# Thirty instead of twenty-six pairs of an up projection by seven products, with nine plain pairs spread among them

## The chip, the cores and the metric

The kernel runs on one core of one Trainium2 chip. The metric is device time in microseconds (us) of one execution, median over runs: 2329.23 us for the kernel before (3 runs, 2329.02 to 2341.73). The engines are called by their short names: PE (TensorE, matmul; PEld is its weight load), DVE (VectorE), ACT (ScalarE), POOL (GpSimd), SP (SyncE, which here issues all DMAs).

## The reference

One decoder block over 512 tokens of width 2048: a modulated RMS norm, two token mixers with a shared output projection, then a gated MLP with a causal depthwise convolution of width 3, and a last norm. The change concerns the MLP's up projection alone:

```python
def _conv_ffn(h, w_up, conv_w, conv_b, w_down):
    T = h.shape[1]
    u = h @ w_up
    up = jnp.pad(u, ((0, 0), (CONV_WIDTH - 1, 0), (0, 0)))
    y = conv_b
    for j in range(CONV_WIDTH):
        y = y + conv_w[j] * up[:, j:j + T]
    val, gate = jnp.split(y, 2, axis=-1)
    return (jax.nn.silu(gate) * val) @ w_down
```

`h` is 512 x 2048, `w_up` is 2048 x 11264, `w_down` 5632 x 2048, all float32.

## The kernel before

All activations are kept transposed: 128 channels on the partitions, 512 tokens on the free axis. A product of float32 precision is made from three matmuls in a narrower format (`mm3`, lines 127 to 130): weight and activation are each split into a high part (a rounding cast, on ACT) and a low part (the difference, on DVE), and high by high, high by low and low by high are summed in PSUM. `split_weights` (lines 117 to 125) does this for a tile of 128 x 512 weights: one load on SP (`wraw`, 4 buffers), one cast (`whi`, 3 buffers, line 122), one difference (`wlo`, 3 buffers, line 124). `project` uses it for four k-tiles at a time.

The up projection has 44 pairs. A pair is 128 columns of the value half and 128 of the gate half. Each goes through `conv` (one ACT instruction and two on DVE, lines 851 to 853), then the gate's Silu on ACT (857), a product on DVE (858) and a store to `actd` in DRAM (859). They are made in three ways:

- the first NORD = 5 pairs in the ordinary way, before the stage in question;
- the next NSEV = 26 pairs by Strassen's seven products in place of eight (in the form with few additions). Tokens are halved (2 x 256), the contraction is halved (2 x 1024), and the pair's two column tiles are the third halving. The sums of the activations are made once (`token_sums`, `token_split`). The weights come in NPC = 4 chunks a pair, each of 2 k-tiles of each half;
- the last 13 pairs are plain ones, made by the generator `plain_tiles`: a pair is two tiles, a tile four quarters of four k-tiles, and `yield` stands after each quarter. A quarter is 12 matmuls of 512 columns. After a tile's fourth quarter its `conv` follows, after a pair's second tile the gate.

The stage is one loop over n, the NST = 4 x NSEV chunks (lines from 1032 on). In each turn it makes the sums of the next chunk's weights on POOL (`weight_sums`, lines 971 to 973), splits the next chunk's plain parts (`parts("p", ...)`: `ph` on ACT, line 983, `pl` on DVE, line 984), loads the raw weights of the chunk after it (line 965, 512 KB, 2 buffers), and splits this chunk's sums (`sh`, `sl`, the same lines), which are put behind the plain parts on ACT and DVE by `issue_after`. All these tiles have 2 buffers. Then PE makes three products on plain parts, one plain quarter, and the four products on sums; each product of a chunk is 6 matmuls of 256 columns. After a pair's fourth chunk `combine` (one ACT and seven DVE instructions, lines 998 to 1005) joins the seven results, and `gated` follows.

PSUM has eight banks of one pool: a pair's seven products take one each, the plain tile in progress one. Two tags are shared: the sums of the weights lie in `wraw` and `wlo` buffers. The order of instructions on each engine is fixed at compile time by a scheduler that follows the order in the program but moves an instruction that is ready ahead of one that is not; on the chip each engine takes its queue in that order.

Behind the stage stands the down projection: it loads the activations back (`ald`, from `actd`), and weights through `split_weights` (`wdn`), and reloads the residual tiles x from DRAM (line 1069, `x<-x2d`, into memory that the stage gives back).

The line that decides where a plain quarter goes is in the loop:

```python
        if n >= 2:
            next(others, None)
```

With 104 chunks and 104 quarters, each chunk from the third on has one, and the two that are left follow the loop.

Of the kernel before, what the change touches and what calls it, by code (L numbers as in the profile page):

```python
# [18 lines left out]
P = 128  # L19
T = 512  # L20
D = 2048
KT = D // P
NF = 44
# [5 lines left out]
WC = 512  # L29
# [2 lines left out]
Q = float(np.exp(-0.5))  # L32
WINS = (2, 4, 8, 16)
NORD = 5
NSEV = 26
NPC = 4
DK = 4

# [26 lines left out]
def block_kernel(ctx, tc, a, out, stop=None, dbg=None):  # L65
# [66 lines left out]
    def project(ps, src, acts, start=True, stop=True, engs=(V,)):  # L132

        n = len(acts)
        for k0 in range(0, n, WC // P):
            nk = min(WC // P, n - k0)
            wh, wl = split_weights(src[:, k0 * P : (k0 + nk) * P], engs[k0 // 4 % len(engs)])
            for kk in range(nk):
                k = k0 + kk
                sl = slice(kk * P, (kk + 1) * P)  # L140
                last = mm3(ps, wh[:, sl], wl[:, sl], *acts[k], start=start and k == 0, stop=stop and k == n - 1)
            beats.append(last.ins)
        return last
# [662 lines left out]
    def bank():  # L806
        return psm.tile([P, T], F32, tag="b", name="b")

    def half(acts, hf):
        sl = slice(hf * HT, (hf + 1) * HT)  # L810
        return [(h[:, sl], l[:, sl]) for h, l in acts]
# [37 lines left out]
    def conv(c, j, tag):  # L849
        y = rb.tile([P, T], F32, tag=tag, name=tag, bufs=2)  # L850
        S.activation(y, c, AF.Identity, bias=col("cb", j), scale=col("cw", 176 + j))
        V.scalar_tensor_tensor(y[:, 1:T], c[:, 0 : T - 1], col("cw", 88 + j), y[:, 1:T], op0=ALU.mult, op1=ALU.add)
        V.scalar_tensor_tensor(y[:, 2:T], c[:, 0 : T - 2], col("cw", j), y[:, 2:T], op0=ALU.mult, op1=ALU.add)
        return y

    def gate_pair(j, yv, yg):
        S.activation(yg, yg, AF.Silu)
        V.tensor_mul(yv, yv, yg)
        nc.sync.dma_start(actd[j], yv)

    def gated(j, cv, cg):
        gate_pair(j, conv(cv, j, "t0"), conv(cg, NF + j, "t1"))
# [100 lines left out]
    def load_four(n):  # L963
        raw = up.tile([P, 4, W2], F32, tag="raw", name="raw", bufs=2)
        nc.sync.dma_start(raw, a["wups"][n // NPC, n % NPC, :, :, :])
        return raw

    def weight_sums(raw):
        sa = wp.tile([P, WC], F32, tag="wraw", name="sums", bufs=4)[:, :].rearrange("p (n w) -> p n w", n=2)
        sb2 = wp.tile([P, WC], F32, tag="wlo", name="sums", bufs=3)[:, :].rearrange("p (n w) -> p n w", n=2)  # L970
        G.tensor_tensor(sa, raw[:, 1:3, :], raw[:, 0:1, :].to_broadcast([P, 2, W2]), op=ALU.add)  # L971
        G.tensor_tensor(sb2[:, 0, :], sa[:, 0, :], raw[:, 2, :], op=ALU.add)  # L972
        G.tensor_tensor(sb2[:, 1, :], sb2[:, 0, :], raw[:, 3, :], op=ALU.add)
        return sa, sb2

    def parts(tag, srcs):
        m = sum(t.shape[1] for t in srcs)
        hi = up.tile([P, m, W2], F32R, tag=tag + "h", name=tag + "h", bufs=2)
        lo = up.tile([P, m, W2], F32R, tag=tag + "l", name=tag + "l", bufs=2)
        n = 0  # L980
        for t in srcs:
            sl = slice(n, n + t.shape[1])
            act = S.copy(hi[:, sl, :], t)  # L983
            dve = V.tensor_tensor(lo[:, sl, :], t, hi[:, sl, :].bitcast(F32), op=ALU.subtract)  # L984
            n += t.shape[1]
        return [(hi[:, i, :], lo[:, i, :]) for i in range(m)], (act, dve)

    def product(q, c, w, xs_):
        for i in range(2):
            sl = slice(i * P, (i + 1) * P)  # L990
            mm3(q, w[0][:, sl], w[1][:, sl], *xs_[i], start=c == 0 and i == 0, stop=c == NPC - 1 and i == 1)

    def combine(q):
        cv = up.tile([P, T], F32, tag="cv", name="cv")
        cg = up.tile([P, T], F32, tag="cg", name="cg")
        u = up.tile([P, 3, HT], F32, tag="u", name="u")
        A1, B1 = slice(0, HT), slice(HT, T)
        S.copy(cg[:, A1], q[1])
        V.tensor_tensor(cv[:, A1], cg[:, A1], q[2], op=ALU.add)
        V.tensor_tensor(u[:, 0, :], cg[:, A1], q[6], op=ALU.subtract)  # L1000
        V.tensor_tensor(u[:, 1, :], u[:, 0, :], q[7], op=ALU.add)
        V.tensor_tensor(u[:, 2, :], u[:, 0, :], q[5], op=ALU.subtract)
        V.tensor_tensor(cg[:, B1], q[5], u[:, 1, :], op=ALU.subtract)
        V.tensor_tensor(cv[:, B1], u[:, 2, :], q[3], op=ALU.add)
        V.scalar_tensor_tensor(cg[:, A1], u[:, 1, :], -1.0, q[4], op0=ALU.mult, op1=ALU.subtract)
        return cv, cg

    def plain_tiles():
        for j in range(NORD + NSEV, NF):
            yv = None  # L1010
            for i in range(2):
                ps = bank()
                for k0 in range(0, KT, WC // P):
                    k1 = k0 + WC // P
                    project(ps, a["wup"][2 * (j - NSEV) + i - 4, :, k0 * P : k1 * P], H2[k0:k1],
                            start=k0 == 0, stop=k1 == KT)
                    if k1 == KT:
                        y = conv(ps, j + NF * i, f"t{i}")
                        if i:
                            gate_pair(j, yv, y)  # L1020
                        yv = y
                    yield

    NST = NSEV * NPC
    others = plain_tiles()
    raws = [load_four(0), load_four(1)]
    sums = weight_sums(raws[0])
    pw, _ = parts("p", [raws[0][:, 1:4, :]])
    q = {}
    for n in range(NST):  # L1030
        c = n % NPC
        if n + 1 < NST:
            raw = raws.pop()
            nsums = weight_sums(raw)
            npw, marks = parts("p", [raw[:, 1:4, :]])
            if n + 2 < NST:
                raws.append(load_four(n + 2))
        with tc.issue_after(marks[0].ins), tc.issue_after(marks[1].ins):
            sw, _ = parts("s", sums)
        (a22, a11, a12), (s1, s3, s2, s4) = pw, sw  # L1040
        ks = (2 * c, 2 * c + 1)
        b11, b21, b22 = half([H2[k] for k in ks], 0), half([H2[k + HK] for k in ks], 0), half([H2[k + HK] for k in ks], 1)
        t1, t2, t3, t4 = ([TK[k][i] for k in ks] for i in range(4))
        if c == 0:
            q = {}
        for m, w, xs_ in ((1, a11, b11), (2, a12, b21), (4, a22, t4)):
            if c == 0:
                q[m] = bank()[:, 0:HT]
            product(q[m], c, w, xs_)
        if n >= 2:  # L1050
            next(others, None)
        for m, w, xs_ in ((6, s2, t2), (7, s3, t3), (5, s1, t1), (3, s4, b22)):
            if c == 0:
                q[m] = bank()[:, 0:HT]
            product(q[m], c, w, xs_)
        if c == NPC - 1:
            gated(NORD + n // NPC, *combine(q))
        if n + 1 < NST:
            sums, pw = nsums, npw
# [102 lines left out]
def pack(x, c, w_ada, b_ada, norm1_g, w_in, mu_shift, w0, w2, a0, a2, g2, k_k, k_a, r_k, ln_x_w, ln_x_b,  # L1162
# [49 lines left out]
    def ftiles(w):  # L1212
        k, n = w.shape
        return C(w.reshape(k // P, P, n // P, P).transpose(2, 1, 0, 3)).reshape(n // P, P, k)

    o["wout"] = ftiles(C(A(w_out[0]).reshape(KT, P, D)[MIX_ORDER]).reshape(D, D))
    wu = A(w_up[0]).reshape(D, 2, NF, P).transpose(0, 2, 1, 3).reshape(D, 88 * P)
    n0, n1 = 2 * NORD * P, 2 * (NORD + NSEV) * P
    o["wup"] = ftiles(np.concatenate([wu[:, 4 * P : n0], wu[:, n1:]], 1))
    wq = wu[:, n0:n1].reshape(2, NPC, 2, P, NSEV, 2, P)  # L1220
    o["wups"] = C(wq[(0, 1, 0, 1), :, :, :, :, (1, 1, 0, 0)].transpose(4, 1, 3, 0, 2, 5)).reshape(
        NSEV, NPC, P, 4, 2 * P)
    o["wup0"] = C(wu[:, : 4 * P]).reshape(KT, P, 4 * P)
# [43 lines left out]
```

## Time and profile before

| | us |
|---|---|
| median of 3 runs | 2329.23 |
| the profiled execution | 2332.65 |
| its span, first to last instruction | 2330.9 |
| PE busy in the span | 2202.7 |
| DVE busy | 1512.6 |
| ACT busy | 925.9 |
| POOL busy | 403.3 |
| the stage of chunks and plain quarters, within the span | 1014.53 to 1823.85 |
| mean granted clock of PE over the span | 0.982 |

An instruction's row has its start, its duration, engine, line, operation, the tile it writes and those it reads, and in brackets the idle time of its engine before it with what ended it. Matmuls overlap, so what one costs is read from the distance between two starts. A group's row has the number of instructions, their busy time and the mean of one in ns, and then the idle time before them by what ended it. Tiles carry their names in the program: `hh` and `hl` are the activations' high and low parts, `tk` those of the sums of activations, `ah` and `al` the down projection's activations.

### The profile page before, as it was taken

What the parts mean: (1) busy time and instruction counts of PE and PEld (TensorE: products, weight loads), DVE (VectorE), ACT (ScalarE), POOL (GpSimd) and SP (SyncE); (2) the same over time, 40 slices, a digit from 0 to 9 for tenths busy, and PEclk for the clock granted to TensorE, in tenths of its full rate; (3) what the DMA queues carried; (4) which work ended last, traced back from release to release, by engine and by line L of the source; (5) the groups of instructions that cost most, each with busy time, mean ns of one, the idle gap of its engine ahead of it and who ended that gap; (6) DMA issues with size and microseconds to landing.
All of it is one profiled execution on the core that took longest, in us unless ns stands there. A gap on an engine that the chain in (4) does not pass through costs nothing.

```text
span 2330.9 us, 41813 instructions
## 1 busy us (share of the span) xinstructions
PE 2202.7 (95%) x16306; PEld 1878.0 (81%) x16306; DVE 1512.6 (65%) x2536; ACT 925.9 (40%) x1551; POOL 403.3 (17%) x390
## 2 busy tenths in 40 slices
PE   7999898888879898999999999999999999999997
PEld 5776666565657798899999999999999788888887
DVE  7896767685865669776656666656666444464457
ACT  4435242332523255544344434443444333343333
POOL 0000000000000005634434333344343000000000
PEclk9999999999989999999999999999999999999999
DMA  9884556566655775433333333333333766666555
GB/s 348 301 307 132 164 181 184 166 202 197 209 177 171 266 224 166 149 108 119 123 109 123 109 115 112 110 117 122 109 122 105 232 202 200 198 199 205 163 165 177
DMA packets 197465, 401.41 MB, mean 172 GB/s; under 512 B 37521, under 2 KB 49553, under 8 KB 193041
## 3 DMA queue, kind: packets, MB, share of 16 engines
q1 hardware_dynamic: 197266, 398.73, 54.0%
q8 instruction: 128, 2.10, 0.4%
q14 instruction: 71, 0.58, 0.1%
HBM read 364.56 MB, written 34.09 MB: 171 GB/s over the span
## 4 chain that ended last, share of the span: by engine, by line
PE 60%; DVE 2%; DMA 2%; ACT 0%; issue 0%; SPq 0%; DVEq 0%; ACTq 0%
PE b L130 20%; PE b L128 20%; PE b L129 20%; DVE wlo L124 1%; DMA wraw<-wdn 1%; DMA wraw<-wout 1%; DVE hl L159 0%; DVE x L1089 0%; ACT whi L122 0%; DVE acc L819 0%; DMA ald<-actd 0%; DVE h L157 0%; DMA x<-part 0%; DMA x<-x2d 0%; DVE x L823 0%
## 5 line engine op out<-in xcount | busy, mean ns | idle before, releaser
L122 ACT CAST whi<-wraw 128x512 fp32r<-128x512 f32 (+1 forms) x594 | 360.4, 609 | 820.8 <-DMA wraw<-wup 254.8
L124 DVE TENSOR_TENSOR wlo<-wraw,whi 128x512 fp32r<-128x512 f32 (+1 forms) x578 | 406.5, 705 | 270.9 <-ACT whi L122 263.1
L128 PE MATMUL b<-ah,whi 128*128 128x512 f32 (+1 forms) x980 | 350.0, 357 | 8.2 <-ACT whi L122 7.3
L130 PE MATMUL b<-ah,wlo 128*128 128x512 f32 (+1 forms) x980 | 349.5, 357 | 6.0 <-DVE wlo L124 5.8
L129 PE MATMUL b<-al,whi 128*128 128x512 f32 (+1 forms) x980 | 348.7, 356 | 0.0
L130 PE MATMUL b<-hh,wlo 128*128 128x512 f32 (+1 forms) x640 | 237.8, 372 | 6.0 <-DVE wlo L124 5.8
L128 PE MATMUL b<-hh,whi 128*128 128x512 f32 (+1 forms) x640 | 238.2, 372 | 0.0
L129 PE MATMUL b<-hl,whi 128*128 128x512 f32 (+1 forms) x640 | 237.8, 372 | 0.0
L128 PEld LDWEIGHTS b<-ah,whi 128*128 128x128 f32 x980 | 186.0, 190 | 36.6 <-ACT whi L122 10.8
L130 PEld LDWEIGHTS b<-ah,wlo 128*128 128x128 f32 x980 | 186.0, 190 | 34.4 <-DVE wlo L124 7.7
L129 PEld LDWEIGHTS b<-al,whi 128*128 128x128 f32 x980 | 186.1, 190 | 26.0
L984 DVE TENSOR_TENSOR pl<-raw,ph 128x768 fp32r<-128x768 f32 x104 | 105.4, 1014 | 153.0 <-ACT ph L983 153.0
L128 PE MATMUL mm<-ah,whi 128*128 128x512 f32 x444 | 183.3, 413 | 10.1 <-ACT whi L122 10.1
L130 PE MATMUL mm<-ah,wlo 128*128 128x512 f32 x444 | 183.8, 415 | 3.2 <-DVE wlo L124 3.2
L129 PE MATMUL mm<-al,whi 128*128 128x512 f32 x444 | 182.4, 411 | 0.0
L972 POOL TENSOR_TENSOR sums<-sums,raw 128x256 f32<-128x256 f32 x104 | 107.5, 1033 | 417.0 <-DVE sl L984 411.1
L130 PE MATMUL b<-tk,sl 128*128 128x256 f32 x624 | 176.7, 283 | 0.0
L129 PE MATMUL b<-tk,sh 128*128 128x256 f32 x624 | 176.5, 283 | 0.0
L128 PE MATMUL b<-tk,sh 128*128 128x256 f32 x624 | 176.0, 282 | 0.0
L983 ACT CAST ph<-raw 128x768 fp32r<-128x768 f32 x104 | 86.3, 830 | 165.9 <-PE b L129 159.5
L381 DVE SCALAR_TENSOR_TENSOR war<-war,cq 128x1024 f32<-128x1024 f32 x96 | 116.9, 1220 | 47.3 <-DMA war<-ada 47.2
L971 POOL TENSOR_TENSOR sums<-raw 128x512 f32<-128x512 f32 x104 | 135.8, 1305 | 66.9 <-DMA raw<-wups 33.1
(277 smaller groups left out, 4699.8 us busy)
## 6 DMA issues: line engine op xcount, KB each, us to landing
raw<-wups SPq DMA_DIRECT2D x104, 512.0 KB, 3.5
war<-ada SPq DMA_DIRECT2D x96, 512.0 KB, 4.4
wraw<-wdn SPq DMA_DIRECT2D x192, 256.0 KB, 3.2
wraw<-wup SPq DMA_DIRECT2D x160, 256.0 KB, 3.6
wa<-ada SPq DMA_DIRECT2D x32, 1024.0 KB, 7.5
wraw<-win SPq DMA_DIRECT2D x108, 256.0 KB, 4.1
ald<-actd SPq DMA_DIRECT2D x88, 256.0 KB, 2.7
wraw<-wout SPq DMA_DIRECT2D x78, 256.0 KB, 4.2
```

The costliest lines, as they stand in the source:

```text
L122: mark[0] = S.copy(hi[:, 0:w], raw[:, 0:w]).ins
L124: mark[1] = eng.tensor_tensor(lo[:, 0:w], raw[:, 0:w], hi[:, 0:w].bitcast(F32), op=ALU.subtract).ins
L128: PE.matmul(ps, wh, xh, start=start, stop=False)
L129: PE.matmul(ps, wh, xl, start=False, stop=False)
L130: return PE.matmul(ps, wl, xh, start=False, stop=stop)
L381: op = V.scalar_tensor_tensor(wa, wa, 1.0, cq[0], op0=ALU.mult, op1=ALU.mult, accum_out=modq[:, kq, j : j + 1])
L971: G.tensor_tensor(sa, raw[:, 1:3, :], raw[:, 0:1, :].to_broadcast([P, 2, W2]), op=ALU.add)
L972: G.tensor_tensor(sb2[:, 0, :], sa[:, 0, :], raw[:, 2, :], op=ALU.add)
L983: act = S.copy(hi[:, sl, :], t)
L984: dve = V.tensor_tensor(lo[:, sl, :], t, hi[:, sl, :].bitcast(F32), op=ALU.subtract)
```

## The change

NSEV goes from 26 to 30, so 30 pairs are made by seven products (120 chunks) and 9 are plain (72 quarters). A chunk has a plain quarter when a count of 72 spread evenly over 120 steps up at it: of every five chunks the second, the fourth and the fifth. The last quarter falls into the last chunk, so none is left after the loop. The weights are packed accordingly on the host, by the same constants.

```diff
 NORD = 5
-NSEV = 26
+NSEV = 30
...
     NST = NSEV * NPC
+    NPLAIN = (NF - NORD - NSEV) * 2 * KT * P // WC
...
-        if n >= 2:
+        if (n + 1) * NPLAIN // NST > n * NPLAIN // NST:
             next(others, None)
```

## The prediction

> **What bounds the kernel now.** I read the page first: the span, the busy shares and the chain that ended last.
>
> ```profile
> span 2330.9 us, 41813 instructions
> PE 2202.7 (95%) x16306; PEld 1878.0 (81%) x16306; DVE 1512.6 (65%) x2536; ACT 925.9 (40%) x1551; POOL 403.3 (17%) x390
> PE 60%; DVE 2%; DMA 2%; ACT 0%; issue 0%; SPq 0%; DVEq 0%; ACTq 0%
> ```
>
> TensorE is busy for 95% of the span, and the chain runs along it. The change touches one stage only, the interleaved stage of seven-product chunks and plain quarters. I found its edges in the timeline of PE: the first matmul on a `ph` tile at 1014.53 and the first one of the down projection (`ah`) at 1823.85. The table of windows says this of it (columns: PE, PEld, DVE, ACT and POOL busy, the granted clock, the DMA share, GB/s):
>
> ```profile
> 1014.53:1823.85 809.32, 809.32 (x5617) 758.12 (x5616) 508.00 (x795) 341.69 (x562) 315.06 (x306) 1.00 0.36 116
> ```
>
> PE has no idle time at all in these 809.3 us, at full clock; DVE is at 63%, ACT at 42%, POOL at 39%. So the stage is what PE's queue holds, and what it holds is read from the starts of its pieces in PE's timeline:
>
> ```profile
> 1400.43 0.40 PE L128 MATMUL b<-hh,whi 128*128 128x512 f32 x1
> ...
> 1403.17 0.28 PE L128 MATMUL b<-tk,sh 128*128 128x256 f32 x1
> ...
> 1406.05 0.28 PE L128 MATMUL b<-hh,ph 128*128 128x256 f32 x1
> ...
> 1408.21 0.40 PE L128 MATMUL b<-hh,whi 128*128 128x512 f32 x1
> ...
> 1415.99 0.40 PE L128 MATMUL b<-hh,whi 128*128 128x512 f32 x1
> ```
>
> A plain quarter (12 matmuls of 512 columns) takes 1403.17 - 1400.43 = 2.74 us. The four products on sums (24 matmuls of 256 columns) take 2.88, the three on plain parts (18) take 2.16: 5.04 us for a chunk. Start to start that is 0.228 us for a wide and 0.120 us for a narrow matmul; the 0.40 and 0.28 of the rows overlap. The check: 104 x (5.04 + 2.74) = 809.1, against 809.3 in the window. The next period, to 1415.99, is 7.78 again.
>
> **The change, the arithmetic.** A seven-product pair is 4 chunks, 20.16 us of PE. A plain pair is 8 quarters, 21.92 us. Four pairs move from the second kind to the first: 16 chunks more (+80.6 us), 32 quarters fewer (-87.7 us): **-7.0 us** while PE has no gap. The bytes do not change: a pair's weights are 4 loads of 512 KB or 8 of 256 KB.
>
> One rule would forbid this trade, and a row bears on it:
>
> ```profile
> L128 PEld LDWEIGHTS b<-tk,sh 128*128 128x128 f32 x624 | 119.4, 191 | 4.0
> ```
>
> Every matmul has its own weight load, whose row says 191 ns, longer than the 120 ns between narrow matmuls. Were the loads to set the narrow pace, a chunk would be 42 x 0.191 = 8.0 us. The 104 chunks already there run at 5.04, so loads overlap, and this keeps a chance of 1%. The Trainium skill (TensorE: Matmul & The Clock Gate, "Back-to-back issue gap") holds that load and matmul together set the spacing in a stream, 81 ns at 128 columns and 131 at 512. Read linearly that is 98 ns at 256, an estimate from that page, and by it a seven-product pair (16.4 us) would cost 3.9 us more than a plain one (12.6), some 16 us more in all. The trace has 120 and 228 instead, and the measurement decides.
>
> **The other engines' work.** Mean ns of one, from the groups by form:
>
> ```profile
> L984 DVE TENSOR_TENSOR sl<-sums,sh 128x512 fp32r<-128x512 f32 x208 | 137.6, 702 | 4.2 <-ACT sh L983 4.1
> L971 POOL TENSOR_TENSOR sums<-raw 128x512 f32<-128x512 f32 x104 | 135.8, 1305 | 66.9 <-DMA raw<-wups 33.1 <-DVE wlo L124 16.9 <-issue 4.8
> L983 ACT CAST sh<-sums 128x512 fp32r<-128x512 f32 x208 | 118.4, 616 | 3.3 <-POOL sums L973 3.0 <-POOL sums L971 0.3
> L972 POOL TENSOR_TENSOR sums<-sums,raw 128x256 f32<-128x256 f32 x104 | 107.5, 1033 | 417.0 <-DVE sl L984 411.1 <-PE b L130 5.7
> L984 DVE TENSOR_TENSOR pl<-raw,ph 128x768 fp32r<-128x768 f32 x104 | 105.4, 1014 | 153.0 <-ACT ph L983 153.0
> L983 ACT CAST ph<-raw 128x768 fp32r<-128x768 f32 x104 | 86.3, 830 | 165.9 <-PE b L129 159.5 <-DMA raw<-wups 6.4
> L973 POOL TENSOR_TENSOR sums<-sums,raw 128x256 f32<-128x256 f32 x104 | 77.6, 746 | 8.2
> ```
>
> A chunk asks 2 x 0.702 + 1.014 = 2.4 us of DVE, 2.1 of ACT and 3.1 of POOL, each under a chunk's 5.04 even with no plain quarter in it. So throughput is not in question; the dates are. ACT's `ph` waits on PE (159.5 us in all): ACT runs ahead until a `ph` buffer comes free, when PE ends the third product of a chunk. From that moment the order is `ph`, `pl`, then `sh`, `sl`, then the `wlo` of a plain quarter. Today there is a plain quarter in every chunk from the third on. Afterwards, of five chunks, the first and third have none, so two chunks without one never follow each other, but a chunk that lacks one gives its successor 2.74 us less of notice.
>
> What that does is read from the timelines of DVE and PE, once in mid-pair and once just behind a pair's end:
>
> ```profile
> 1411.23 0.68 DVE L124 TENSOR_TENSOR wlo<-wraw,whi 128x512 fp32r<-128x512 f32 x1
> ...
> 1414.05 0.41 DVE L1004 TENSOR_TENSOR cv<-u,b 128x256 f32<-128x256 f32 x1
> 1415.77 0.75 DVE L852 SCALAR_TENSOR_TENSOR t<-cg,vec,t 128x511 f32<-128x511 f32 x1 [1.31 <-ACT t L851]
> ...
> 1418.47 0.95 DVE L984 TENSOR_TENSOR pl<-raw,ph 128x768 fp32r<-128x768 f32 x1
> 1419.34 0.69 DVE L858 TENSOR_TENSOR t<-t,t 128x512 f32<-128x512 f32 x1
> 1419.94 1.29 DVE L984 TENSOR_TENSOR sl<-sums,sh 128x512 fp32r<-128x512 f32 x2
> 1421.14 0.69 DVE L124 TENSOR_TENSOR wlo<-wraw,whi 128x512 fp32r<-128x512 f32 x1
> ```
>
> ```profile
> 1423.77 0.40 PE L128 MATMUL b<-hh,whi 128*128 128x512 f32 x1
> ...
> 1424.23 0.39 PE L130 MATMUL b<-hh,wlo 128*128 128x512 f32 x1
> ```
>
> In mid-pair `wlo` is done at 1411.91 for a quarter that starts at 1415.99 and reads `wlo` first 0.46 us later: 4.5 us in hand, 1.8 after a chunk without a quarter. No stall. Behind a pair's end the combine and the pair's convolution stand ahead of `pl` and `wlo` on DVE: done at 1421.83, needed at 1424.23, 2.40 us in hand, and 2.74 are taken away: **0.35 us of stall**. That meets the pairs whose first chunk lacks a quarter: numbering chunks from 0, those with n mod 20 equal to 0 or 12, without n = 0 eleven of them. The `sl` of the same place has more notice (done at 1421.23 for products that start 2.74 us behind 1423.77, so 5.3 us now and 2.5 then). Cost: **+3.9 us**; the bounds are 0, if the queue is ordered so that `wlo` goes first, and some 13 by the third rival below.
>
> PSUM banks: seven for a pair and one for the plain tile, eight in all, now as then. At a pair's end the first new products take the banks of products 1 and 2, read early, and DVE frees the next every 0.35 us of the combine, against 0.72 us of PE for a product. I take nothing; the cover is that lead, and without it the third rival follows. At the start the first plain quarter goes into the second chunk instead of the third, a moment earlier in an order that has slack: nothing, within 0.5 us either way. SP issues 16 large loads more and 32 small ones fewer: nothing.
>
> **The end of the stage.** Today the last chunk is followed by two plain quarters, and the last store of an activation and the reloads of x stand on SP's queue ahead of more down weights (rows of PE and of SP):
>
> ```profile
> 1818.38 0.40 PE L128 MATMUL b<-hh,whi 128*128 128x512 f32 x1
> ...
> 1840.57 0.50 PE L128 MATMUL b<-ah,whi 128*128 128x512 f32 x1 [2.96 <-ACT whi L122]
> ...
> 1843.24 0.63 PE L130 MATMUL b<-ah,wlo 128*128 128x512 f32 x1
> 1843.66 0.63 PE L128 MATMUL b<-ah,whi 128*128 128x512 f32 x1
> ```
>
> ```profile
> 1823.71 0.32 SPq L859 DMA_DIRECT2D actd<-t  x1
> 1824.07 2.36 SPq L1069 DMA_DIRECT2D x<-x2d  x5
> 1828.53 0.32 SPq L859 DMA_DIRECT2D actd<-t  x1
> 1828.90 4.47 SPq L1069 DMA_DIRECT2D x<-x2d  x9
> 1833.87 1.67 SPq L120 DMA_DIRECT2D wraw<-wdn  x2
> ```
>
> PE lives on weights loaded before and then waits 2.96 us; for some 3 us after it the matmuls come 0.42 apart, half pace. Afterwards the stage ends on a pair's own products. The last pair's store came 5.33 us behind its end (1823.71 - 1818.38); with a plain tile's convolution beside it, about 6.8. Today the last store is 1828.53 - 1823.85 = 4.68 behind the end. So the wait could grow by 2.1 us, or it could shrink away with the slow stretch behind it (-4.5), since the loads of x also need buffers that come free later, and more down weights may slip ahead. Both ends are unseen; I take **0**.
>
> **Sum**: -7.0 + 3.9 + 0 = -3.1 us. The profiled execution took 2332.65 us (span 2330.9 and 1.75 around it) and would take 2329.5; it stood 3.4 above the median of 2329.23, from which the forecast is counted: **2326.1 us**.
>
> **The rivals.**
> First, no stall in the stage: 2322.2. For it: all other work has slack, and an in-order queue may well carry `wlo` earlier when its date is earlier. Against: DVE's order behind a pair's end, above.
> Second, the wait at the down projection grows: 2326.1 + 2.1 = 2328.2. For it: the store is on the chain. Against: the runway of weights may be longer. The Trainium skill (TensorE: Matmul & The Clock Gate, "The HAM clock gate") says that the clock halves after an idle window of about 3.4 us and needs one busy window to return; the 2.96 us here already cost such a stretch, so a longer idle would add itself alone.
> Third, on the other side: in every twentieth chunk (n mod 20 = 19) a plain tile ends in the very chunk that ends a pair. Its convolution then stands on DVE in front of the combine, where today it falls a chunk later, into idle time:
>
> ```profile
> 1427.53 0.75 DVE L852 SCALAR_TENSOR_TENSOR t<-b,vec,t 128x511 f32<-128x511 f32 x1
> 1428.31 0.75 DVE L853 SCALAR_TENSOR_TENSOR t<-b,vec,t 128x510 f32<-128x510 f32 x1
> ```
>
> That is 1.5 us more at five places that have no slack left, and 0.69 more (the gate's product) at two of them: 5 x 1.5 + 2 x 0.69 = 8.9, so 2335.0. It makes the kernel slower from 0.6 us a place on (3.1 / 5). Against: DVE has idle time before a pair's end that could take it.
> Fourth, narrow matmuls paced by their loads: 16 x 42 x 0.191 - 87.7 = +40.7, 2369.9.
> Fifth, the change does not do what it says, its quarters running out or left for the tail: (n+1) x 72 // 120 steps by one 72 times, so this would leave 2329.2 only by a slip that I do not see.
>
> **How the numbers follow.** Forecast 0.43; no stall 0.25; longer wait 0.13; the two convolutions 0.15; load pace 0.01; no change 0.03. The forecast's own range is 2321 to 2330. The range 2319 to 2335 takes in the first rival with half of what the end could give, and the third; what is left out is the whole gain at the end and heavier stalls, under 2 in 10. A measurement of this kernel tells about 1% (23 us) from no change. Only load pace and a piling up of stalls reach over it above, nothing below: faster 0.01, same 0.96, slower 0.03.
>
> **What would show it.** In the profile after, 30 x 4 chunks of 5.04 us and 72 quarters of 2.74 on PE; the stage 802 us plus its stalls; PE waiting on `wlo` about 0.35 us at eleven places behind a pair's end; the wait of 2.96 before the sixth down weight still there. A stage under 803 us says the first rival, one over 812 the third, a chunk over 5.1 the fourth.

## The result, and the profile after

The changed kernel is slower: 2370.39 us median (2360.13 to 2373.79, 6 runs) against 2334.07 for the kernel before in the same series (2329.02 to 2341.73, 6 runs), ratio 1.0159, 95% interval 1.0140 to 1.0179. The forecast was 2326.1, the range 2319 to 2335.

The page after, the lines that answer to those of before:

```profile
span 2369.3 us, 42436 instructions
PE 2213.9 (93%) x16594; PEld 1899.4 (80%) x16594; DVE 1615.3 (68%) x2580; ACT 939.1 (40%) x1571; POOL 488.2 (21%) x438
PE 23%; DVE 2%; DMA 2%; issue 1%; ACT 0%; SPq 0%; POOL 0%; DVEq 0%; ACTq 0%; POOLq 0%
```

The span is 38.4 us longer. The stage of chunks and quarters, from the first `ph` matmul to the first of the down projection, in the table of windows (columns as in the prediction):

```profile
1015.47:1858.23 842.76, 815.93 (x5905) 776.12 (x5904) 609.12 (x833) 354.14 (x580) 399.99 (x354) 0.99 0.36 111
```

It takes 842.8 us instead of 809.3 (+33.5), and what follows it 2369.3 - 1858.23 = 511.1 instead of 2330.9 - 1823.85 = 507.1 (+4.0): 37.5 of the 38.4. In the stage PE now has 842.76 - 815.93 = 26.8 us of idle time, where it had none. What it waits for there, from the view of waits (total us, times, longest):

```profile
PE b L130 <- DVE sl L984: 23.9, 12, 3.0
PE b L128 <- DVE u L1000: 2.7, 5, 0.9
```

No wait on `wlo` is among them. The twelve waits on `sl` stand at the pairs' first chunks n mod 20 = 8 and 16, six times 2.5 to 3.0 us (n mod 20 = 8) and six times 0.8 to 1.4 (n mod 20 = 16). Those are the pairs that follow on a pair whose last chunk has no plain quarter: n mod 20 = 7 and 15. One of them, at n = 28, on DVE:

```profile
1206.85 0.96 DVE L984 TENSOR_TENSOR pl<-raw,ph 128x768 fp32r<-128x768 f32 x1 [0.99 <-ACT ph L983]
1207.73 0.41 DVE L1001 TENSOR_TENSOR u<-u,b 128x256 f32<-128x256 f32 x1
...
1209.06 0.41 DVE L1005 SCALAR_TENSOR_TENSOR cg<-u,b 128x256 f32<-128x256 f32 x1
1209.39 0.68 DVE L984 TENSOR_TENSOR sl<-sums,sh 128x512 fp32r<-128x512 f32 x1
1210.02 0.75 DVE L852 SCALAR_TENSOR_TENSOR t<-cv,vec,t 128x511 f32<-128x511 f32 x1
1210.73 0.75 DVE L852 SCALAR_TENSOR_TENSOR t<-cg,vec,t 128x511 f32<-128x511 f32 x1
1211.39 1.83 DVE L853 SCALAR_TENSOR_TENSOR t<-cv,vec,t 128x510 f32<-128x510 f32 x1
1213.15 1.21 DVE L853 SCALAR_TENSOR_TENSOR t<-cg,vec,t 128x510 f32<-128x510 f32 x1
1214.28 1.21 DVE L984 TENSOR_TENSOR sl<-sums,sh 128x512 fp32r<-128x512 f32 x1
```

and on PE and POOL at the same time:

```profile
1212.28 0.28 PE L128 MATMUL b<-tk,sh 128*128 128x256 f32 x1
...
1215.54 0.39 PE L130 MATMUL b<-tk,sl 128*128 128x256 f32 x1 [2.75 <-DVE sl L984]
...
1216.52 0.41 PE L128 MATMUL b<-tk,sh 128*128 128x256 f32 x1
1216.74 0.41 PE L129 MATMUL b<-tk,sh 128*128 128x256 f32 x1
```

```profile
1211.39 1.29 POOL L971 TENSOR_TENSOR sums<-raw 128x512 f32<-128x512 f32 x1 [7.06 <-DMA raw<-wups]
1212.64 1.17 POOL L972 TENSOR_TENSOR sums<-sums,raw 128x256 f32<-128x256 f32 x1
1213.88 1.05 POOL L973 TENSOR_TENSOR sums<-sums,raw 128x256 f32<-128x256 f32 x1
```

Three things are to be seen. DVE is never idle between 1206.85 and the end of the last `sl` at 1215.49, so PE waits for a queue, not for a dependency of `sl`. The queue's order is another than before: the combine and all four instructions of the convolution stand ahead of the last `sl`, where before `sl` and `wlo` came first and the combine after them (`wlo` at 1411.23, the combine's last at 1414.05 in the prediction's rows). And rows that take 0.74 and 0.68 us by themselves take 1.83, 1.21 and 1.21 while POOL is at work on the next sums. Behind this wait PE runs at 0.21 us a narrow matmul instead of 0.12, as it does behind five of the six long ones.

The end of the stage, on PE and SP:

```profile
1860.17 0.33 SPq L859 DMA_DIRECT2D actd<-t  x1
...
1865.97 0.32 SPq L859 DMA_DIRECT2D actd<-t  x1
1866.34 7.71 SPq L1070 DMA_DIRECT2D x<-x2d  x13
...
1875.07 0.33 SPq L120 DMA_DIRECT2D wraw<-wdn  x1
```

```profile
1881.90 0.79 PE L128 MATMUL b<-ah,whi 128*128 128x512 f32 x1 [4.44 <-ACT whi L122]
```

The last store comes 1865.97 - 1858.23 = 7.7 us behind the stage (4.7 before), and PE's wait at the down projection grew from 2.96 to 4.44. By PE's timeline the down projection's 61st high-by-high matmul starts 48.0 us behind the stage's end, 46.0 before, and the 601st 415.2 against 413.2. So 2.0 of the 4.0 us are lost at the head of the down projection. The other 2.0 lie in the last 96 us, where the change alters nothing, and where the runs below differ among each other by as much (93.2 to 96.4 us).

### The profile page after: what moved, and what is told of

Read it like the earlier page. It is cut to its first block, busy times and chain, and to the rows that moved or that the text cites. A ratio compares the mean times of both kernels' runs of the same rounds, so it can differ in the third digit from the quotient of the medians.

```text
span 2369.3 us, 42436 instructions
## 1 busy us (share of the span) xinstructions
PE 2213.9 (93%) x16594; PEld 1899.4 (80%) x16594; DVE 1615.3 (68%) x2580; ACT 939.1 (40%) x1571; POOL 488.2 (21%) x438
## 5 line engine op out<-in xcount | busy, mean ns | idle before, releaser
L122 ACT CAST whi<-wraw 128x512 fp32r<-128x512 f32 (+2 forms) x562 | 340.3, 608 | 668.0 <-PE b L129 242.1
L124 DVE TENSOR_TENSOR wlo<-wraw,whi 128x512 fp32r<-128x512 f32 (+2 forms) x546 | 395.4, 727 | 290.4 <-ACT whi L122 278.6
L984 DVE TENSOR_TENSOR pl<-raw,ph 128x768 fp32r<-128x768 f32 x120 | 133.0, 1108 | 148.3 <-ACT ph L983 148.1
L130 PE MATMUL b<-tk,sl 128*128 128x256 f32 x720 | 208.3, 289 | 24.1 <-DVE sl L984 23.9
L971 POOL TENSOR_TENSOR sums<-raw 128x512 f32<-128x512 f32 x120 | 170.6, 1422 | 204.7 <-DMA raw<-wups 141.0
L984 DVE TENSOR_TENSOR sl<-sums,sh 128x512 fp32r<-128x512 f32 x240 | 205.7, 892 | 2.9 <-ACT sh L983 2.7
L129 PE MATMUL b<-tk,sh 128*128 128x256 f32 x720 | 206.2, 287 | 0.0
L128 PE MATMUL b<-tk,sh 128*128 128x256 f32 x720 | 205.5, 286 | 0.1
L130 PE MATMUL b<-hh,wlo 128*128 128x512 f32 (+1 forms) x512 | 187.1, 365 | 7.8 <-DVE wlo L124 7.7
L128 PE MATMUL b<-hh,whi 128*128 128x512 f32 (+1 forms) x512 | 186.8, 365 | 0.0
L129 PE MATMUL b<-hl,whi 128*128 128x512 f32 (+1 forms) x512 | 186.5, 364 | 0.0
```

Source lines behind the costliest of these rows:

```text
L122: mark[0] = S.copy(hi[:, 0:w], raw[:, 0:w]).ins
L124: mark[1] = eng.tensor_tensor(lo[:, 0:w], raw[:, 0:w], hi[:, 0:w].bitcast(F32), op=ALU.subtract).ins
L128: PE.matmul(ps, wh, xh, start=start, stop=False)
L129: PE.matmul(ps, wh, xl, start=False, stop=False)
L130: return PE.matmul(ps, wl, xh, start=False, stop=stop)
```

## The experiments

**Theory A**: where a pair's last chunk has no plain quarter, the combine and the convolution are ready 2.74 us earlier against the next chunk's `sl`, the compile-time order puts them ahead, and PE waits at the next pair's first chunk. **Rival B**: it is the short chunk as such, wherever it stands, because DVE and POOL cannot keep its pace. Each kernel is compared with the kernel before on its chip (median 2326.2 or 2326.7 there). The stage is from each run's own trace.

| kernel | stage us | PE idle in it | DVE busy in it | ratio to before (95%) |
|---|---|---|---|---|
| before | 809.3 | 0 | 508.0 | 1 |
| the change | 842.8 | 26.8 | 609.1 | 1.0159 (1.0140 to 1.0179) |
| spread rule, 26 pairs | 809.1 | 0 | 491.8 | 1.0012 (0.9997 to 1.0027) |
| 30 pairs, last chunk has a quarter | 815.8 | 9.3 | 566.7 | 1.0030 (1.0018 to 1.0041) |
| 30 pairs, last chunk has none | 878.0 | 55.5 | 643.1 | 1.0322 (1.0304 to 1.0339) |
| the change, convolution behind `sl` | 817.5 | 10.0 | 610.4 | 1.0049 (1.0034 to 1.0064) |
| the change without the sums on POOL | 802.1 | 0 | 508.4 | 0.9975 (0.9956 to 0.9995) |
| 30 pairs, old rule | 829.1 | 18.5 | 574.1 | 1.0090 (1.0070 to 1.0110) |
| 31 pairs, second and fourth chunk | 800.9 | 0.4 | 618.4 | 0.9970 (0.9953 to 0.9988) |
| the same, reloads of x later | 801.1 | 0.5 | 618.6 | 0.9954 (0.9936 to 0.9972) |

**The spread rule alone.**

```diff
-NSEV = 30
+NSEV = 26
```

> 26 pairs as before, only the rule that spreads the quarters: each of the 104 chunks has one, from the first on, and none is left behind the loop. Theory A (the stalls come where a pair's last chunk has no plain quarter, because DVE's queue then has the combine and the convolution ahead of the next chunk's last sl) and rival B (any chunk without a quarter is too short for the slowed DVE and POOL) both expect a stage without PE waits, 809 us. What it measures is the stage's end alone: PE's wait at the down projection grows from 2.96 to about 4.4 us, and the kernel comes out some 4 us (0.2%) above the one before.

The stage is as long as before and without waits. What remains of the rule is the end: one wait behind it, on `whi`, of 3.8 us (some 4.4 expected, 2.96 before, 4.44 in the change). The ratio cannot be told from 1; the 4 us expected (1.0017) lie within its interval.

**The last chunk of a pair always with a quarter, and never.**

```diff
-        if (n + 1) * NPLAIN // NST > n * NPLAIN // NST:
+        if c in (1, 3) or c == 2 and (n // NPC + 1) * 12 // NSEV > n // NPC * 12 // NSEV:
```

> 30 pairs and 72 quarters as in the change, but placed by the pair: the second and the fourth chunk of each pair always have a quarter, and the third in 12 of 30. Still 48 chunks have none, never two in a row, only no pair's last chunk is among them. Theory A: no wait of PE on sl at a pair's first chunk; stage 802 to 806 us instead of 843, the kernel about 3 us below the one before (ratio 0.998 to 1.000). Rival B: 48 short chunks as in the change, so about the same 33 us of waits, ratio 1.016. The prediction's own term (wlo late by 0.35 us where the first chunk lacks a quarter) would now meet 29 pairs: 10 us, ratio 1.002 to 1.004.

```diff
-        if (n + 1) * NPLAIN // NST > n * NPLAIN // NST:
+        if c in (0, 2) or c == 1 and (n // NPC + 1) * 12 // NSEV > n // NPC * 12 // NSEV:
```

> 30 pairs and 72 quarters, the first and the third chunk of each pair always have one, the second in 12 of 30, the last never. Theory A: PE waits on sl behind each of 29 pair ends, by 1.5 to 4.2 us with the slow stretch (the two sizes of the change), so 43 to 120 us in the stage, ratio 1.02 to 1.05. Rival B: 48 chunks without a quarter as in the change, ratio 1.016.

Both have 48 chunks without a quarter, as the change has. The view of waits of PE in the stage, first where the last chunk always has one, then where it never has:

```profile
PE b L128 <- DVE u L1000: 8.9, 12, 1.2
PE b L130 <- DVE sl L984: 0.2, 1, 0.2
```

```profile
PE b L130 <- DVE sl L984: 55.5, 29, 3.4
```

One wait on `sl` against 29, one for each pair end, in the two sizes of the change. The two kernels differ in a pair's first chunk as well, which never has a quarter in one and always in the other. DVE's rows tell the two apart: the last `sl` of a new pair stands behind the combine at 29 of 29 pair ends in the second kernel, at 12 in the change and at none in the first or before, each time exactly where the last chunk has no quarter. In the change the pairs at n mod 20 = 4 have a quarter in both chunks and no wait on `sl`. With the old rule, below, pairs without one in either chunk wait. So the place of the last chunk's quarter decides, and B in its plain form falls. Theory A was not wholly right on the first: 12 waits of some 0.7 us for a PSUM bank were not expected (the third product of a new pair waits until DVE's first subtraction has read an old bank, and mostly behind pairs with three quarters that instruction stands behind `pl`, `sl` and `wlo`). They make the stage 815.8 instead of at most 806. The prediction's term, `wlo` late in the second chunk, would have cost 10 us here; there is no wait on `wlo` at all.

**The change with the convolution queued behind `sl`.**

```diff
+        if late:
+            with tc.issue_after(smarks[1].ins):
+                gated(NORD + n // NPC - 1, *late)
+            late = None
...
-            gated(NORD + n // NPC, *combine(q))
+            late = combine(q)
```

> The change with its own places for the quarters, but a pair's convolution and gate are traced one turn later and queued on DVE behind the next chunk's last sl. Theory A: the waits of PE on sl (24 us now) fall under 3, the stage takes 803 to 810 us, ratio 0.998 to 1.002 against the kernel before. Rival B: the chunks are as short as before, the waits stay near 24 us, ratio 1.013 to 1.016.

```profile
PE b L130 <- DVE wlo L124: 4.0, 6, 0.8
PE b L130 <- DVE sl L984: 3.2, 6, 1.2
PE b L128 <- DVE u L1000: 2.8, 1, 2.8
```

The waits on `sl` fall from 23.9 to 3.2 us with the quarters where the change has them, and none is left at a pair's first chunk; 25 us of the stage are won by order alone, while DVE is as busy as in the change (610 us). What is left is `wlo`, which now stands behind the convolution, one wait for a bank, and a remnant on `sl` in second chunks. The expected 803 to 810 us are missed by 7, and the ratio of 1.0049 lies above the expected 0.998 to 1.002.

**The change without the sums on POOL.**

```diff
     def weight_sums(raw):
+        t = cmat[:, :, :].rearrange("p (n i) w -> p n (i w)", n=2)
+        return t, t
...
```

> The change, but the sums of the weights are left out: POOL does nothing in the stage, and the splits of sums read a constant tile of the same shape. DVE's queue keeps its order at the pair ends that matter (combine, the first sl, four instructions of the convolution, the last sl). If the queue's order alone makes the waits, they stay at 2.9 and 1.4 us. If POOL's work beside DVE's stretches them (rows of 0.75 us took 1.8, of 0.68 took 1.2 while POOL ran), the DVE chain ahead of the last sl gets 1.6 to 2.1 us shorter: 0.8 and 0 us are left, some 5 us of waits on sl in all instead of 24, and the stage takes 804 to 810 us instead of 843.

The same place, n = 28, DVE (line 988 is the splits' line here):

```profile
1193.44 0.95 DVE L988 TENSOR_TENSOR pl<-raw,ph 128x768 fp32r<-128x768 f32 x1
...
1195.96 0.69 DVE L988 TENSOR_TENSOR sl<-cmat,sh 128x512 fp32r<-128x512 f32 x1
1196.60 0.75 DVE L852 SCALAR_TENSOR_TENSOR t<-cv,vec,t 128x511 f32<-128x511 f32 x1
1197.31 0.75 DVE L852 SCALAR_TENSOR_TENSOR t<-cg,vec,t 128x511 f32<-128x511 f32 x1
1197.97 0.74 DVE L853 SCALAR_TENSOR_TENSOR t<-cv,vec,t 128x510 f32<-128x510 f32 x1
1198.64 0.74 DVE L853 SCALAR_TENSOR_TENSOR t<-cg,vec,t 128x510 f32<-128x510 f32 x1
1199.30 0.68 DVE L988 TENSOR_TENSOR sl<-cmat,sh 128x512 fp32r<-128x512 f32 x1
```

The order is the bad one, `sl` last, and PE does not wait: the last `sl` ends at 1199.98, and the first matmul that reads it starts without a gap:

```profile
1199.97 0.28 PE L128 MATMUL b<-tk,sh 128*128 128x256 f32 x1
...
1200.20 0.28 PE L130 MATMUL b<-tk,sl 128*128 128x256 f32 x1
```

The stage is 802.1 us, the whole of the predicted gain, with no wait at all where some 5 us were expected. From the `pl` at the head of the queue to the end of the last `sl` DVE takes 6.54 us here and 8.64 in the change (1206.85 to 1215.49). Those 2.1 us are three stretched rows: 1.83 + 1.21 + 1.21 against 0.74 + 0.74 + 0.68.

They are not all that this run takes away. The `pl` starts 6.53 us ahead of the four products here and 5.43 in the change, where it waits for its `ph`, and ACT has put a plain quarter's `whi`, which waits for its load, ahead of that `ph`:

```profile
1205.47 0.62 ACT L122 CAST whi<-wraw 128x512 fp32r<-128x512 f32 x1 [0.73 <-DMA wraw<-wup]
1205.99 0.83 ACT L983 CAST ph<-raw 128x768 fp32r<-128x768 f32 x1
```

So at n = 28 the last `sl` comes 3.2 us later against the four products than in this run, 2.1 by stretched rows and 1.1 by the late `ph`. The late `ph` stands at all six places with n mod 20 = 8. At those with n mod 20 = 16 `pl` starts 6.53 us ahead as here, and the stretch alone makes the shorter waits; this is what the two sizes are. The bad order without either uses up the slack to 0.2 us. Without the sums, their buffers and POOL's dates are gone too, so this run by itself does not hold POOL's use of memory apart from all else; that the rows lengthen beside POOL's is read from the rows, in the last section.

**Thirty pairs with the old rule.**

```diff
-        if (n + 1) * NPLAIN // NST > n * NPLAIN // NST:
+        if n >= 2:
```

> 30 pairs with the old rule: a quarter in every chunk from the third on until the 72 are used up (chunk 73), then 46 chunks with none. Theory A: no wait of PE on sl up to chunk 75, then one at each of 11 pair ends, 1.4 to 4.2 us each: 16 to 46 us in the stage, ratio 1.005 to 1.017. Rival B (short chunks as such, wherever they are): waits inside pairs too from chunk 74 on, not only at their ends, and as large a sum as in the change.

```profile
PE b L130 <- DVE sl L984: 18.5, 32, 1.6
```

Apart from half a us in the second chunk there is no wait until the quarters are used up, then waits follow each of the 11 pair ends. Their sum is within Theory A's 16 to 46 us and below the 23.9 of the change that B asked for. They are up to 1.6 us at the first late `sl`, as A has it, and behind ten of the eleven two more of 0.2 to 0.4 us in the next chunk, where DVE has not caught up, which A did not expect. That much of rival B is right: without quarters a late start is not made good within one chunk. Inside pairs, apart from these, there is no wait. The spread of the change is worse than this (1.0159 against 1.0090), although it spreads the quarters evenly.

**A placement built on the theory, and the end.**

```diff
-NSEV = 30
+NSEV = 31
...
-        if (n + 1) * NPLAIN // NST > n * NPLAIN // NST:
+        if c % 2 and n >= 2:
```

> 31 pairs by seven products and 8 plain ones; a quarter in the second and fourth chunk of every pair from the first pair's fourth chunk on, so every pair but none of the first chunks ends with one, every plain tile ends in a second chunk, and 3 quarters are left behind the loop. Theory A: DVE's queue has sl and wlo ahead of the combine at all pair ends; no waits in the stage, 124 x 5.03 + 64 x 2.75 = 800 us, and the end as before; 9 us under the kernel before (ratio 0.996). Rival B: 63 chunks without a quarter, more waits than in the change, ratio above 1.01.

The stage is 800.9 us with 0.3 us of waits, as expected, and the ratio 0.9970 is below 1 beyond its interval. DVE's rows are stretched as in the change (an `sl` takes 883 ns in the mean against 889, a `wlo` 1029 against 851), yet nothing waits except 0.3 us in the stage's second chunk, since `sl` stands ahead of the combine at every pair's end. Stretching without the bad order costs nothing here, nor does the bad order once POOL's sums, and with them the late `ph`, are gone.

```diff
-        t = rx.tile([P, T], F32, tag=f"x2_{f}", name=f"x2_{f}")
-        nc.sync.dma_start(t, x2d[f])
-        x2.append(t)
+        x2.append(rx.tile([P, T], F32, tag=f"x2_{f}", name=f"x2_{f}"))
...
             down(pss[f], f, k0, DK, A, k0 == 0, k0 + DK == NF)
+            if k0 in (2 * DK, 3 * DK):
+                i = f + (k0 // DK - 2) * NB
+                with tc.issue_after(xdma):
+                    nc.sync.dma_start(x2[i], x2d[i])
+            xdma = beat_dma[-1]
```

(`beat_dma` collects the weight loads in `split_weights`.)

> The same with the 16 reloads of x moved from the head of the down projection into its third and fourth round of weights. If the reloads on SP's queue, held by the last stores, are what delays the down weights, PE's wait of 3 us at the start of the down projection and the slow stretch behind it (1.5 us) go: some 4 to 5 us under the same kernel without this (ratio 0.994). If the loads themselves are late, the wait stays.

PE has no wait left from the stage's end to 1900 us (3.9 in the kernel above, 2.96 before). So the reloads of x on SP's queue did delay the down weights. In the profiled executions what follows the stage takes 501.3 us instead of 509.3. The two intervals overlap, so the 4 us between the two ratios are not secured by the times; against the kernel before the gain is.

## Why the prediction was wrong

- **What bounds the kernel**: right. The stage was PE's alone, and is again whenever nothing is late.
- **The arithmetic, -7.0 us**: right. Without waits the change's stage takes 802.07 instead of 809.32, -7.2. The load pace of 0.191 us did not come about.
- **The step that failed is "what that does"**, the one that priced the shorter notice at 3.9 us. The stage lost 842.76 - 802.07 = 40.7 us: 26.8 of idle PE and 13.9 of longer PE time (815.93 busy against 802.07), most of it slower matmuls behind the long waits. Three things in it were wrong. It took the rows around 1411 for mid-pair, where they are a pair's end: six of the combine's seven DVE rows stand there, from 1411.87 to 1414.46, and the products on sums at 1418.73 are the new pair's first. So it priced `wlo` at this place, and the `sl` only one chunk later. It took DVE's order from the trace of before and moved only the date at which PE needs each tile; but that order is made at compile time from when each instruction can start, and moving a quarter on PE moves the combine in DVE's queue. The same holds for ACT's queue and the late `ph`. And it took the durations of DVE's rows as fixed, while they depend on whether POOL reads memory at the same time. Before, the last `sl` at such a place was done 7.4 us ahead of the four products:

```profile
1410.03 1.28 DVE L984 TENSOR_TENSOR sl<-sums,sh 128x512 fp32r<-128x512 f32 x2
```

```profile
1418.73 0.28 PE L128 MATMUL b<-tk,sh 128*128 128x256 f32 x1
```

  Less 2.74 that would have left 4.7 us; instead PE waited 2.75 us for it at n = 28.
- **The place**: the eleven first chunks without a quarter have no wait on `wlo`: there `wlo` is now ready ahead of the combine. The twelve places that do wait are those behind a last chunk without a quarter, which the text called free of stalls.
- **The end, 0**: the head of the down projection lost 2.0 us, where the second rival had 2.1, and that rival's mechanism was the right one (a later last store, 7.7 against its 6.8 us; the wait longer by 1.5). "More down weights may slip ahead" did not happen.
- **The third rival** had the right engine and the right sign, the convolution ahead in DVE's queue, but the wrong chunks: at n mod 20 = 19 it named 8.9 us, and there are five waits for a bank of 2.7 in all, three of them behind those chunks. The range's upper end was built on it. A stage over 812 us was to be its sign; 842.8 us came about in another way, so that sign did not tell the rivals apart.
- **The fourth rival**: its 2369.9 us is half a us from the measured 2370.4 by chance alone. A chunk was not slower where nothing waits: the four products take 2.87 us there, 2.88 before.
- **The chance of slower by over 1%** was 0.03, put on load pace and "a piling up of stalls"; the stalls were all priced with before's order, so none of them could reach it.

## What to carry to other kernels

When an edit moves work on one engine, do not read the other engines' queues from the old trace as if they stood still: a compile-time order may flip wherever two instructions become ready in another sequence, and a tile with 5 us in hand can come 3 us late. Where a pipeline closes a group (here a pair's combine), keep the filler work at the closing step, and see that the next group's inputs stand ahead of the closing work in the queue (an explicit edge won 25 us of the stage here; the placement of the 31-pair kernel leaves 0.3 us of waits). Even spacing is not the aim by itself: the change spreads its quarters as evenly as their number allows and waits; the 31-pair kernel has one in every second chunk, in step with the pairs.

## What the runs showed of the hardware

Some DVE instructions are stretched by POOL's, and which ones is seen in the groups. The change, in the stage:

```profile
L984 DVE TENSOR_TENSOR sl<-sums,sh 128x512 fp32r<-128x512 f32 x238 | 203.3, 889 | 0.0
L853 DVE SCALAR_TENSOR_TENSOR t<-cv,vec,t 128x510 f32<-128x510 f32 x29 | 33.6, 1157 | 0.0
L853 DVE SCALAR_TENSOR_TENSOR t<-b,vec,t 128x510 f32<-128x510 f32 x19 | 14.2, 745 | 0.5
L1001 DVE TENSOR_TENSOR u<-u,b 128x256 f32<-128x256 f32 x30 | 12.4, 414 | 1.3
```

and without POOL's sums:

```profile
L988 DVE TENSOR_TENSOR sl<-cmat,sh 128x512 fp32r<-128x512 f32 x238 | 154.1, 685 | 0.0
L853 DVE SCALAR_TENSOR_TENSOR t<-cv,vec,t 128x510 f32<-128x510 f32 x29 | 21.6, 744 | 0.0
```

With both inputs in SBUF (`sl`, and the convolution of `cv`) the mean goes from 685 to 889 and from 744 to 1157 ns; with one input in a PSUM bank (`b`) it stays at 745 and 414, although 16 of the 19 and 15 of the 30 rows run beside a POOL row. In the change too, the 14 of the 29 `cv` rows on line 853 that no POOL row meets take 744 ns in the mean. In all, the same work takes 609 us of DVE instead of 508.

The Trainium skill (SBUF — State Buffer, "Who interferes with whom") says that a DVE instruction with two SBUF inputs contends with a GpSimd instruction that reads SBUF, that the ports they share are an exclusive lock, and that the order of issue decides who is held up. The trace agrees: a row of 0.74 us that starts together with a POOL row of 1.29 takes 1.83. Before, the order was mostly the other way. The `wlo` at 1411.23 in the prediction's rows keeps its 0.68 us, and the POOL row that starts inside it takes 1.06, where the next one of the same shape takes 0.74:

```profile
1411.46 1.06 POOL L972 TENSOR_TENSOR sums<-sums,raw 128x256 f32<-128x256 f32 x1 [4.11 <-DVE sl L984]
1412.59 0.74 POOL L973 TENSOR_TENSOR sums<-sums,raw 128x256 f32<-128x256 f32 x1
```

Waits of PE of 2.7 to 3.0 us were followed in the change by matmuls at nearly half pace for some microseconds (granted clock 0.86 in the 12.3 us from 1207.37, by the row below). The sixth long wait, 2.50 us at n = 88, was not, nor were those of about 1.3 us (1.00 around n = 16). The length alone does not decide it: where the last chunk never has a quarter, 8 of 12 waits of 2.65 to 3.44 us were followed by such a stretch, and one of 3.18 was not.

```profile
1207.37:1219.65 12.28, 9.53 (x57) 8.84 (x55) 11.39 (x17) 4.41 (x7) 4.74 (x5) 0.86 0.31 96
1128.00:1136.00 8.00, 6.73 (x47) 6.13 (x46) 8.00 (x8) 2.62 (x5) 5.66 (x5) 1.00 0.19 42
```

So a wait twice as long could cost three times as much: from the start of the four products to the next chunk's, PE's timeline has 4.40 us at n = 16 (1130.23 to 1134.63) and 7.37 at n = 28 (1212.28 to 1219.65), against 2.87 without a wait.
